# Fourteen projection panels computed channel-major in a hybrid attention/SSD/delta-rule layer

## The chip, the cores and the metric

The kernel runs on one core of one Trainium2 chip. The metric is the device time of one execution in microseconds (us). Engines are named as the profile names them: PE is TensorE, with PEld for its weight loads; DVE is VectorE; ACT is ScalarE; POOL is GpSimd; SP issues the weight DMAs. In a matmul the *stationary* operand (up to 128 columns) is loaded into the array first, and the *moving* operand (up to 512 columns) streams past it.

## The reference

One layer with three groups of heads, on 256 tokens of width 4096 (float32):

```python
h = rms_norm(x, norm_w)
proj = einsum('bsd,de->bse', h, w_in)               # 4096 -> 14392
(fox_qkv, fox_f, fox_z, ssd_xbc, ssd_z, ssd_dt, gdn_qkv, gdn_z, gdn_beta, gdn_a) = split(proj)
o_fox = forgetting attention of fox_qkv, gated by silu(fox_z)
xbc = silu(causal_depthwise_conv(ssd_xbc, ssd_conv_w) + ssd_conv_b)   # 4 taps along the tokens
o_ssd = chunked state-space scan of xbc, gated by silu(ssd_z)
qkv = silu(causal_depthwise_conv(gdn_qkv, gdn_conv_w))                # 4 taps along the tokens
o_gdn = chunked gated delta rule of qkv, gated by silu(gdn_z)
return x + concat(o_fox, o_ssd, o_gdn) @ w_out
```

The causal convolution works on each channel by itself: out[t] = w3 x[t] + w2 x[t-1] + w1 x[t-2] + w0 x[t-3].

## The kernel before

**The projection.** The 14392 output columns are 28 panels of 512 (`UNITS`) and 56 narrow gate columns. The contraction over 4096 has 32 steps `k` (`KT`) of 128. Operands are float32, split into a high and a low part in float32r (fp32r), which the PE takes in one pass; a product is then three matmuls: high x high, low x high, high x low. The input is split once into 32 tiles `xhl[k]` of [128 channels, 2 parts, 256 tokens]. The weights arrive by SP's queue, two steps in a DMA, and are split step by step: ACT writes `wh` (`split_w`, L189), DVE writes `wl` (L190); each has five buffers. In `product` (L193) the stationary operand is a [128 channels, 128 tokens] piece of `xhl[k]` and the moving one the 512 weight columns. So a panel's result stands token-major in two PSUM banks of [128 tokens, 512 channels], one for each half of the tokens.

**Panels.** `first_panels` (L243) does the first two panels (gq0, gk0) and the gate columns together, while the input still arrives. Each further panel is one call of `panel` (L204). The bank pool `psproj` has three banks, a panel uses two. When a panel is done, `take` (L936) reads both banks out on ACT, with the tokens' factor `rstd` of the RMS norm as a factor for each partition, and `unit_done` puts the panel's further work, a generator, into the queue `prep`. `panel` calls `drive` after each step, which lets the generators go on by one piece: so the later stages (convolution, attention, scans) are strewn among the products of the next panels. Last come eight output panels (`wo`) by the same `panel`, with `mix_split` for its left operand; they aren't touched. A scheduler decides from the program's order and its own estimate the order on each engine; on the chip each engine goes through its list in order.

**The convolution.** 14 of the 28 panels go through `conv_unit` (L389): gq, gk, gv of three groups, sB, sC and three sx. As the panel is token-major and the convolution runs along the tokens, eight 128x128 transposes on the PE (L397) first turn it into channel-major form in PSUM (`cps`). Then, for each of four channel tiles, ACT multiplies by the last tap (L404) and DVE adds the three shifted products (L407), both reading PSUM.

**The norm.** `input_norm` (L292), behind the first two panels, sums the squares over the channels by one matmul (`xnps`) and gets `rstd` by a chain of small DVE operations. `take` of the first panels waits for it.

Of the kernel before, what the change touches and what calls it, by code (L numbers as in the profile page):

```python
# [19 lines left out]
P = 128  # L20
D = 4096
T = 256
# [65 lines left out]
def tile_hybrid(ctx: ExitStack, tc: tile.TileContext, x, xT, w, wo, prm, cst, lev, out):  # L88
# [52 lines left out]
    def split_tile(k, name):  # L141
        return cp.tile([P, 2, T], F32R, tag=f"xhl{k}", name=f"{name}{k}")

# [49 lines left out]
    def product(ps, t, wh, wl, k):  # L193

        for tb in range(2):
# [3 lines left out]
            nc.tensor.matmul(ps[tb], h, wl, start=False, stop=k == KT - 1)  # L199

    def w_tile():
        return wp.tile([P, CK, 512], F32, tag="wr", name="wr", bufs=4)

    def panel(src, lhs):  # L204

        ps = [pp.tile([P, 512], F32, tag="proj", name="proj") for _ in range(2)]
        for c in range(0, KT, CK):
            wr = w_tile()
            nc.sync.dma_start(out=wr, in_=src[:, c:c + CK, :])
            for j in range(CK):  # L210
                wh, wl = split_w(wr[:, j, :])
                product(ps, lhs(c + j), wh, wl, c + j)
                drive()
        return ps

    def gate_chunk(ps, k0):

        n = GK_STEP
        gr = t2([P, n, NG], name="gwr")
        nc.sync.dma_start(out=gr, in_=w[0:P * WG].rearrange("(p j n) -> p j n", p=P, n=NG)[:, k0:k0 + n, :])  # L220
        gw = r4([P, n, 2 * NG], F32R, name="gw", tag="raw")
        nc.scalar.copy(gw[:, :, 0:NG], gr)
        nc.vector.tensor_tensor(out=gw[:, :, NG:2 * NG], in0=gr, in1=gw[:, :, 0:NG].bitcast(F32), op=ALU.subtract)
        for j in range(n):
            k = k0 + j
            nc.tensor.matmul(ps[0:2 * NG, :], gw[:, j, :], xhl[k].rearrange("p a t -> p (a t)"),  # L226
                             start=k == 0, stop=k == KT - 1)

    def gate_columns(ps):

        gs = t2([P, 2, T], name="gsum")
        nc.scalar.copy(gs[0:2 * NG, :, :], ps[0:2 * NG, :].rearrange("p (a t) -> p a t", a=2))
        o = bank("gtok")
        for tb in range(2):
            for i in range(2):
                nc.tensor.matmul(o[:, tb * NG:tb * NG + NG], gs[0:2 * NG, i, tb * P:tb * P + P],
                                 cst_s[0:2 * NG, M_GS:M_GS + NG], start=i == 0, stop=i == 1)
        raw["gates"] = cp.tile([P, 2, NG], F32, name="graw")
        for tb in range(2):
            nc.scalar.activation(raw["gates"][:, tb, :], o[:, tb * NG:tb * NG + NG], AF.Copy,  # L240
                                 scale=st["rstd"][:, tb:tb + 1])

    def first_panels(srcs):  # L243
# [4 lines left out]
        for c in range(0, KT, CK):  # L248
# [9 lines left out]
            for j in range(CK):  # L258
# [7 lines left out]
                for i in range(len(srcs)):  # L266
                    wh, wl = split_w(wr[i][:, j, :])
                    product(ps[i], xhl[k], wh, wl, k)
            if (c + CK) % GK_STEP == 0:
# [22 lines left out]
    def input_norm():  # L292
# [8 lines left out]
        affine(ss, v4(ps[:, 0:T], 2)[:, :, 0], 1.0 / D, EPS)  # L301
        st["rstd"] = rsqrt(ss, 2, "xn", 1)

    def const_tiles():
# [12 lines left out]
    def gates():  # L317
# [32 lines left out]
                                       op0=ALU.max, op1=ALU.add)  # L350
        ga = cp.tile([P, 2, NSP], F32, name="ga")
        nc.vector.tensor_tensor(out=ga, in0=spl, in1=mid(ea, 2), op=ALU.mult)
# [36 lines left out]
    def conv_unit(src, cw, dst, bias=None):  # L389

        acc = r4([P, 4, T], name="acc")
        for pr in range(2):
            ps = bank("cps")
            for i in range(2):
                ct = 2 * pr + i
                for tb in range(2):
                    nc.tensor.transpose(ps[:, i * T + tb * P:i * T + tb * P + P],  # L397
                                        src[:, tb, ct * P:ct * P + P], ident)
            for i in range(2):
                ct = 2 * pr + i  # L400
                q = ps[:, i * T:(i + 1) * T]
                wc = [prm_s[:, cw + ct * 4 + j:cw + ct * 4 + j + 1] for j in range(4)]
                b = 0.0 if bias is None else prm_s[:, bias + ct:bias + ct + 1]
                nc.scalar.activation(acc[:, ct, :], q, AF.Identity, scale=wc[3], bias=b)  # L404
                for j in (2, 1, 0):
                    s = 3 - j
                    nc.vector.scalar_tensor_tensor(out=acc[:, ct, s:], in0=q[:, 0:T - s], scalar=wc[j],  # L407
                                                   in1=acc[:, ct, s:], op0=ALU.mult, op1=ALU.add)
                yield 2
        if isinstance(dst, list):  # L410
# [522 lines left out]
    def unit_src(i):  # L933
        return w[P * (WG + i * WU):P * (WG + (i + 1) * WU)].rearrange("(p j n) -> p j n", p=P, n=512)

    def take(i, ps):  # L936
        name = UNITS[i][0]
        raw[name] = r4([P, 2, 512], name=f"raw_{name}", tag="raw")
        for tb in range(2):
            nc.scalar.activation(raw[name][:, tb, :], ps[tb], AF.Copy, scale=st["rstd"][:, tb:tb + 1])  # L940
        unit_done(name)
# [8 lines left out]
    for i in range(2, len(UNITS)):  # L950
        take(i, panel(unit_src(i), lambda k: xhl[k]))

# [72 lines left out]
```

## Time and profile before

| | before |
|---|---|
| time, median of 3 runs | 1756.83 us (1756.27 to 1756.95) |
| the profiled execution | 1756.48 us; its span, first to last instruction, 1754.7 us |
| PE busy | 1743.5 us, 99% |
| PEld (weight loads) busy | 1437.4 us, 82% |
| DVE busy | 1129.4 us, 64% |
| ACT busy | 954.5 us, 54% |
| granted PE clock | 1.00 |

Busy time is the time in which at least one instruction of the engine was under way. Matmuls overlap in the array, so a matmul's duration is longer than the distance to the next one; where the price of a matmul is wanted, starts are compared. Weight loads overlap matmuls and one another.

### The profile page before, as it was taken

Reading aid. Unit: us, or ns where it says so; the run is one execution under the profiler, and the core shown is the slowest. Engines: PE = TensorE matmul, PEld = TensorE weight load, DVE = VectorE, ACT = ScalarE, POOL = GpSimd, SP = SyncE. Lnnn points to the kernel's source line nnn. Section 1 sums busy time; section 2 is a strip of 40 time slices with the busy share of each in tenths; the row PEclk is TensorE's granted clock in tenths of the full one; section 3 lists DMA queues with packets and bytes.
Section 4 is the critical chain, followed back from the end, with each engine's and each line's share of the span. In section 5 each row is a group of like instructions: output and inputs, shape, how many; then the busy total and the mean of one; then the engine's idle time right before and its main releaser. Section 6 shows DMA issues by size and latency. Waiting matters only on the chain.

```text
span 1754.7 us, 24331 instructions
## 1 busy us (share of the span) xinstructions
PE 1743.5 (99%) x8368; PEld 1437.4 (82%) x8368; DVE 1129.4 (64%) x2111; ACT 954.5 (54%) x1678; POOL 133.3 (8%) x124
## 2 busy tenths in 40 slices
PE   8999999999999999999999999999999999999999
PEld 6888888888888888888888888888888888888887
DVE  8567767677677677575666765555655665555554
ACT  8456655455555555455555655556555754444443
POOL 0000200002000110002324100010000000000000
PEclk9999999999999999999999999999999999999999
DMA  8655555555555555555555566665666577777674
GB/s 318 187 169 181 161 174 156 157 170 159 175 147 163 159 170 166 146 168 166 169 168 162 175 191 182 190 182 168 181 190 182 172 235 215 215 215 214 202 204 138
DMA packets 90267, 317.73 MB, mean 181 GB/s; under 512 B 10016, under 2 KB 11040, under 8 KB 90144
## 3 DMA queue, kind: packets, MB, share of 16 engines
q1 hardware_dynamic: 83808, 302.94, 58.4%
q10 hardware_dynamic: 6336, 13.24, 2.1%
q8 instruction: 65, 1.06, 0.2%
q14 instruction: 58, 0.48, 0.1%
HBM read 311.95 MB, written 4.19 MB: 180 GB/s over the span
## 4 chain that ended last, share of the span: by engine, by line
PE 99%; ACT 0%; DMA 0%; DVE 0%; issue 0%; ACTq 0%
PE proj L197 30%; PE proj L199 30%; PE proj L198 30%; PE cps L397 1%; PE kkps L543 1%; PE yp L746 1%; PE yps L523 0%; PE zps L523 0%; PE zqs L523 0%; PE gproj L226 0%; PE mps L435 0%; PE cor L523 0%; PE o L523 0%; PE atps L523 0%; PE vn L523 0%; PE dps L383 0%
## 5 line engine op out<-in xcount | busy, mean ns | idle before, releaser
L190 DVE TENSOR_TENSOR wl<-wr,wh 128x512 fp32r<-128x512 f32 x1152 | 817.8, 720 | 539.6 <-ACT wh L189 479.2
L189 ACT CAST wh<-wr 128x512 fp32r<-128x512 f32 x1152 | 708.5, 621 | 705.3 <-DVE wl L190 362.1
L197 PE MATMUL proj<-wh,xhl 128*128 128x512 f32 x1792 | 710.5, 397 | 6.8 <-ACT wh L189 6.8
L198 PE MATMUL proj<-wh,xhl 128*128 128x512 f32 x1792 | 705.5, 394 | 0.0
L199 PE MATMUL proj<-wl,xhl 128*128 128x512 f32 x1792 | 693.5, 395 | 0.0
L197 PEld LDWEIGHTS proj<-wh,xhl 128*128 128x128 f32 x1792 | 337.4, 188 | 77.4 <-ACT wh L189 7.6
L198 PEld LDWEIGHTS proj<-wh,xhl 128*128 128x128 f32 x1792 | 337.4, 188 | 71.0
L199 PEld LDWEIGHTS proj<-wl,xhl 128*128 128x128 f32 x1792 | 336.6, 188 | 71.1
L197 PE MATMUL proj<-wh,mhl 128*128 128x512 f32 x512 | 200.8, 393 | 0.5 <-ACT wh L189 0.5
L198 PE MATMUL proj<-wh,mhl 128*128 128x512 f32 x512 | 199.9, 391 | 0.0
L199 PE MATMUL proj<-wl,mhl 128*128 128x512 f32 x512 | 196.5, 392 | 0.0
L197 PEld LDWEIGHTS proj<-wh,mhl 128*128 128x128 f32 x512 | 96.2, 188 | 21.6 <-ACT wh L189 1.2
L199 PEld LDWEIGHTS proj<-wl,mhl 128*128 128x128 f32 x512 | 96.2, 188 | 21.4
L198 PEld LDWEIGHTS proj<-wh,mhl 128*128 128x128 f32 x512 | 96.2, 188 | 21.1
L407 DVE SCALAR_TENSOR_TENSOR acc<-cps,prm_s,acc 128x255 f32<-128x255 f32 (+2 forms) x168 | 75.6, 476 | 9.5 <-ACT acc L404 8.8
L377 POOL TENSOR_TENSOR G<-cst_s,gh 128x384 fp32r<-128x384 f32 (+1 forms) x22 | 20.8, 947 | 230.3 <-DVE gh L354 120.5
L404 ACT ACTIVATE acc<-cps,prm_s 128x256 f32<-128x256 f32 x56 | 27.5, 510 | 13.9 <-PE cps L397 7.7
L588 DVE TENSOR_TENSOR tn<-tn,zps 128x512 f16<-128x512 f16 (+1 forms) x36 | 24.6, 683 | 4.4 <-PE zps L523 4.4
L597 POOL TENSOR_TENSOR res<-cst_s,tn 128x512 f32<-128x512 f32 x6 | 7.7, 1296 | 240.0 <-DVE tn L588 236.5
L377 POOL TENSOR_TENSOR G<-cst_s,gl 128x384 fp32r<-128x384 f32 (+1 forms) x22 | 25.3, 1152 | 0.2 <-PE dps L383 0.2
L589 DVE TENSOR_TENSOR tt<-tt,zqs 128x512 f16<-128x512 f16 (+1 forms) x36 | 24.5, 681 | 0.0
L579 ACT CAST y<-yps 128x512 f16<-128x512 f32 x36 | 19.4, 587 | 5.0 <-PE yps L523 4.9
(298 smaller groups left out, 935.4 us busy)
## 6 DMA issues: line engine op xcount, KB each, us to landing
wr<-in_w SPq DMA_DIRECT2D x446, 512.0 KB, 3.6
wr<-in_wo SPq DMA_DIRECT2D x128, 512.0 KB, 3.6
xres<-in_x ACTq DMA_DIRECT2D x16, 256.0 KB, 3.3
out<-xres ACTq DMA_DIRECT2D x16, 256.0 KB, 4.1
xr<-in_xT ACTq DMA_DIRECT2D x7, 514.0 KB, 5.2
wr<-in_w SPq DMA_DIRECT2D x4, 256.0 KB, 4.8
gwr<-in_w SPq DMA_DIRECT2D x4, 224.0 KB, 4.8
xr<-in_xT ACTq DMA_DIRECT2D x1, 385.5 KB, 4.6
```

The source lines that it names most:

```text
L189: nc.scalar.copy(wh, wr)
L190: nc.vector.tensor_tensor(out=wl, in0=wr, in1=wh.bitcast(F32), op=ALU.subtract)
L197: nc.tensor.matmul(ps[tb], h, wh, start=k == 0, stop=False)
L198: nc.tensor.matmul(ps[tb], lo, wh, start=False, stop=False)
L199: nc.tensor.matmul(ps[tb], h, wl, start=False, stop=k == KT - 1)
L377: nc.gpsimd.tensor_tensor(out=g[i], in0=mid(U, n), in1=bc(src[:, tb, c0:c0 + n].bitcast(F32), P), op=ALU.mult)
L397: nc.tensor.transpose(ps[:, i * T + tb * P:i * T + tb * P + P], src[:, tb, ct * P:ct * P + P], ident)
L404: nc.scalar.activation(acc[:, ct, :], q, AF.Identity, scale=wc[3], bias=b)
L407: nc.vector.scalar_tensor_tensor(out=acc[:, ct, s:], in0=q[:, 0:T - s], scalar=wc[j], in1=acc[:, ct, s:], op0=ALU.mult, op1=ALU.add)
L579: nc.scalar.copy(y[tb], v4(ps))
L588: nc.vector.tensor_tensor(out=tn2, in0=tn[tb], in1=v4(zp), op=ALU.subtract)
L589: nc.vector.tensor_tensor(out=tt2, in0=tt[tb], in1=v4(zq), op=ALU.subtract)
```

## The change

For the 14 panels that go through the convolution the operands of the product change places: 128 weight columns are stationary and the 256 tokens are moving (`product_t`). A step then has four channel tiles with three matmuls of 256 columns each. The result is channel-major at once: a bank holds two channel tiles of [128 channels, 256 tokens]. The transposes fall away, and the convolution reads the panel from SBUF.

Two things follow. A bank now holds two accumulations side by side. The first matmul of each bank is therefore 512 columns wide: it moves the high part of the tokens and 256 zeros behind it, for which tile 0 of the input has a third, cleared part (`x0z`). And `rstd` is now needed along the free axis: `input_norm` makes it into a row that is the same in all partitions (`rrow`), by scaling the identity on DVE, one fp32 matmul with ones, and a copy on ACT. `take` multiplies the banks by this row on DVE in place of ACT's scaled copy. Some gate tiles move from the constant pool to a rotating one.

```diff
     def split_tile(k, name):
-        return cp.tile([P, 2, T], F32R, tag=f"xhl{k}", name=f"{name}{k}")
+        if k:
+            return cp.tile([P, 2, T], F32R, tag=f"xhl{k}", name=f"{name}{k}")
+        t = cp.tile([P, 3, T], F32R, tag="xhl0", name=f"{name}0")
+        if name == "xhl":
+            nc.vector.memset(t[:, 1, :].bitcast(F32), 0.0)
+            st["x0z"] = t[:, 0:2, :]
+        return t[:, 0:3:2, :]
...
+    def product_t(ps, t, wh, wl, k):
+        xh, xl = t[:, 0, :], t[:, 1, :]
+        for ct in range(4):
+            o = ps[ct // 2][:, ct % 2 * T:ct % 2 * T + T]
+            h, lo = (v[:, ct * P:ct * P + P] for v in (wh, wl))
+            if k == 0 and ct % 2 == 0:
+                nc.tensor.matmul(v4(ps[ct // 2], 2), h, st["x0z"], start=True, stop=False)
+            else:
+                nc.tensor.matmul(o, h, xh, start=False, stop=False)
+            nc.tensor.matmul(o, h, xl, start=False, stop=False)
+            nc.tensor.matmul(o, lo, xh, start=False, stop=k == KT - 1 and ct % 2 == 1)
...
-    def panel(src, lhs):
+    def panel(src, lhs, mul=product):
...
-                product(ps, lhs(c + j), wh, wl, c + j)
+                mul(ps, lhs(c + j), wh, wl, c + j)
...
-                    product(ps[i], xhl[k], wh, wl, k)
+                    product_t(ps[i], xhl[k], wh, wl, k)
...
         st["rstd"] = rsqrt(ss, 2, "xn", 1)
+        dg = t2([P, 2, P], name="rdiag")
+        for tb in range(2):
+            nc.vector.tensor_scalar_mul(dg[:, tb, :], ident, st["rstd"][:, tb:tb + 1])
+        ps = bank("rrow")
+        nc.tensor.matmul(ps[:, 0:T], ones, dg.rearrange("p a b -> p (a b)"), start=True, stop=True)
+        st["rrow"] = cp.tile([P, T], F32, name="rrow")
+        nc.scalar.copy(st["rrow"], ps[:, 0:T])
...
     def conv_unit(src, cw, dst, bias=None):
         acc = r4([P, 4, T], name="acc")
-        for pr in range(2):
-            ps = bank("cps")
-            for i in range(2):
-                ct = 2 * pr + i
-                for tb in range(2):
-                    nc.tensor.transpose(ps[:, i * T + tb * P:i * T + tb * P + P],
-                                        src[:, tb, ct * P:ct * P + P], ident)
...
-                q = ps[:, i * T:(i + 1) * T]
+        for ct in range(4):
+            q = src[:, ct, :]
...
+    CONV = ("gq", "gk", "gv", "sB", "sC", "sx")
+
     def take(i, ps):
         name = UNITS[i][0]
-        raw[name] = r4([P, 2, 512], name=f"raw_{name}", tag="raw")
-        for tb in range(2):
-            nc.scalar.activation(raw[name][:, tb, :], ps[tb], AF.Copy, scale=st["rstd"][:, tb:tb + 1])
+        if name[:2] in CONV:
+            raw[name] = r4([P, 4, T], name=f"raw_{name}", tag="raw")
+            for b in range(2):
+                nc.vector.tensor_tensor(out=raw[name][:, 2 * b:2 * b + 2, :], in0=v4(ps[b], 2), in1=mid(st["rrow"], 2),
+                                        op=ALU.mult)
+        else:
+            raw[name] = r4([P, 2, 512], name=f"raw_{name}", tag="raw")
+            for tb in range(2):
+                nc.scalar.activation(raw[name][:, tb, :], ps[tb], AF.Copy, scale=st["rstd"][:, tb:tb + 1])
...
-        take(i, panel(unit_src(i), lambda k: xhl[k]))
+        take(i, panel(unit_src(i), lambda k: xhl[k], product_t if UNITS[i][0][:2] in CONV else product))
```

How the instructions move is shown at two places. The first is the PE's list in panel gv0, the third panel, whose first bank is served alone for some steps, as the second is still to be read out. A row is a line of the kernel, the operation, out<-in by the program's names, and the columns. Before, one half of the tokens for the steps 0 to 3:

```order
L197 MATMUL proj<-wh,xhl_90 128x512
L198 MATMUL proj<-wh,xhl_90 128x512
L199 MATMUL proj<-wl,xhl_90 128x512
L197 MATMUL proj<-wh,xhl_119 128x512
L198 MATMUL proj<-wh,xhl_119 128x512
L199 MATMUL proj<-wl,xhl_119 128x512
```

After, the first two channel tiles for the steps 0 and 1:

```order
L216 MATMUL proj<-xhl_90,wh 128x512
L219 MATMUL proj<-xhl_90,wh 128x256
L220 MATMUL proj<-xhl_90,wl 128x256
L218 MATMUL proj<-xhl_90,wh 128x256
L219 MATMUL proj<-xhl_90,wh 128x256
L220 MATMUL proj<-xhl_90,wl 128x256
L218 MATMUL proj<-xhl_132,wh 128x256
L219 MATMUL proj<-xhl_132,wh 128x256
L220 MATMUL proj<-xhl_132,wl 128x256
L218 MATMUL proj<-xhl_132,wh 128x256
L219 MATMUL proj<-xhl_132,wh 128x256
L220 MATMUL proj<-xhl_132,wl 128x256
```

Three matmuls of 512 columns have become six of 256, and at step 0 the first of the bank is 512 wide.

The second place is DVE's list when the first two panels go to their convolutions. `wl` is the split of a weight step, `acc` an operation of the convolution, `raw_gq` and `raw_gk` the reading of a bank, `be`, `pre`, `g_ab`, `gl` gate values. Before, where the first operations of the convolution stand:

```order
L357 TENSOR_TENSOR gl<-ga,gh 128x88
L190 TENSOR_TENSOR wl<-wr,wh 128x512 x4
L407 SCALAR_TENSOR_TENSOR acc<-cps,prm_s,acc 128x255 x2
L407 SCALAR_TENSOR_TENSOR acc<-cps,prm_s,acc 128x254 x2
L407 SCALAR_TENSOR_TENSOR acc<-cps,prm_s,acc 128x253
L190 TENSOR_TENSOR wl<-wr,wh 128x512
L407 SCALAR_TENSOR_TENSOR acc<-cps,prm_s,acc 128x253
L190 TENSOR_TENSOR wl<-wr,wh 128x512
```

After, the rows right behind the row of rstd (five steps of gv0 have been split ahead of it):

```order
L326 TENSOR_SCALAR rdiag<-cst_s,xn_y 128x128 x2
L963 TENSOR_TENSOR raw_gq_1444<-proj,rrow 128x512 x2
L963 TENSOR_TENSOR raw_gk_1447<-proj,rrow 128x512 x2
L348 TENSOR_TENSOR pre<-graw,prm_s 128x88
L427 SCALAR_TENSOR_TENSOR acc<-raw_gq_1444,prm_s,acc 128x255 x2
L387 TENSOR_SCALAR be<-be 128x24
L427 SCALAR_TENSOR_TENSOR acc<-raw_gq_1444,prm_s,acc 128x255 x2
L350 TENSOR_SCALAR pre<-pre 128x2x8
L427 SCALAR_TENSOR_TENSOR acc<-raw_gq_1444,prm_s,acc 128x254
L197 TENSOR_TENSOR wl<-wr,wh 128x512
L427 SCALAR_TENSOR_TENSOR acc<-raw_gq_1444,prm_s,acc 128x254
```

The readings of the first two panels have come into DVE's list, and five operations of the convolution stand between them and the next split; five more and two gate operations stand between that split and the one after, three more before the third.

## Rows read from the trace of the kernel before

**Rows 1.** The page: busy time of the engines; the granted clock in 40 slices.

```profile
PE 1743.5 (99%) x8368; PEld 1437.4 (82%) x8368; DVE 1129.4 (64%) x2111; ACT 954.5 (54%) x1678; POOL 133.3 (8%) x124
PEclk9999999999999999999999999999999999999999
```

**Rows 2.** The page: the chain of work that ended last, by line.

```profile
PE proj L197 30%; PE proj L199 30%; PE proj L198 30%; PE cps L397 1%; PE kkps L543 1%; PE yp L746 1%; PE yps L523 0%; PE zps L523 0%; PE zqs L523 0%; PE gproj L226 0%; PE mps L435 0%; PE cor L523 0%; PE o L523 0%; PE atps L523 0%; PE vn L523 0%; PE dps L383 0%
```

**Rows 3.** Groups by line: count, busy us, mean ns, idle before.

```profile
L190 DVE TENSOR_TENSOR wl<-wr,wh 128x512 fp32r<-128x512 f32 x1152 | 817.8, 720 | 539.6 <-ACT wh L189 479.2 <-PE proj L198 25.8 <-PE proj L199 19.6
L197 PE MATMUL proj<-wh,xhl 128*128 128x512 f32 x1792 | 710.5, 397 | 6.8 <-ACT wh L189 6.8
...
5.70 0.80 PE L197 MATMUL proj<-wh,xhl 128*128 128x512 f32 x1 [5.70 <-ACT wh L189]
```

**Rows 4.** Timeline of the PE near 800 us: start, duration; 22 products.

```profile
801.03 0.39 PE L197 MATMUL proj<-wh,xhl 128*128 128x512 f32 x1
...
805.83 0.39 PE L197 MATMUL proj<-wh,xhl 128*128 128x512 f32 x1
```

**Rows 5.** Groups by line and shape: the transposes, one of six groups.

```profile
L397 PE MATMUL cps<-cst_s,raw_sx 128*128 128x128 f32 x24 | 3.9, 272 | 0.0
```

**Rows 6.** Timeline of the PE around one set of four transposes.

```profile
783.52 0.60 PE L397 MATMUL cps<-cst_s,raw_sx 128*128 128x128 f32 x4
...
784.20 0.40 PE L198 MATMUL proj<-wh,xhl 128*128 128x512 f32 x1
```

**Rows 7.** Timeline: weight loads under short matmuls; a run of 128-column fp32 matmuls.

```profile
107.89 1.09 PEld L236 LDWEIGHTS gtok<-cst_s,gsum 112*128 112x128 f32 x8
108.12 1.00 PE L236 MATMUL gtok<-cst_s,gsum 112*128 112x56 f32 x8
108.91 0.19 PEld L197 LDWEIGHTS proj<-wh,xhl 128*128 128x128 f32 x1
...
500.06 1.95 PE L523 MATMUL atps<-tn,m 128*128 128x128 f32 x16
```

**Rows 8.** Timeline of the PE: fp32r matmuls of 384 and 512 columns among products, two in each place.

```profile
851.19 0.34 PE L382 MATMUL dps<-G,slr 128*128 128x384 f32 x1
...
851.54 0.40 PE L197 MATMUL proj<-wh,xhl 128*128 128x512 f32 x1
...
199.52 0.40 PE L382 MATMUL dps<-G,slr 128*128 128x512 f32 x1
...
200.00 0.39 PE L197 MATMUL proj<-wh,xhl 128*128 128x512 f32 x1
```

**Rows 9.** Timeline of the PE: four records of fp32 matmuls of 256 columns.

```profile
189.07 1.02 PE L543 MATMUL kkps<-kq 128*128 128x256 f32 x4
```

**Rows 10.** Groups by line and shape, DVE and ACT.

```profile
L407 DVE SCALAR_TENSOR_TENSOR acc<-cps,prm_s,acc 128x254 f32<-128x254 f32 x56 | 26.3, 476 | 0.2
L153 DVE SCALAR_TENSOR_TENSOR xhl<-xr,xhl 128x256 fp32r<-128x256 f32 x32 | 14.2, 483 | 3.6 <-ACT xhl L152 3.6
L495 DVE TENSOR_TENSOR kn<-kps,rsqk_y 128x512 f32<-128x512 f32 x6 | 3.9, 685 | 0.1
L903 DVE COPY fot<-ofp 128x128 f32<-128x128 f32 x16 | 4.6, 288 | 3.6 <-ACT osq L902 3.6
L447 ACT ACTIVATE mix<-mps,prm_s 128x256 f32<-128x256 f32 x24 | 9.8, 473 | 1.2 <-PE mps L435 1.1
L940 ACT ACTIVATE raw_gk<-proj,xn_y 128x512 f32<-128x512 f32 x6 | 4.0, 693 | 0.6 <-PE proj L199 0.6
```

**Rows 11.** Timeline: the first reading behind the norm, and the PE's next product.

```profile
107.87 1.27 ACT L940 ACTIVATE raw_gq<-proj,xn_y 128x512 f32<-128x512 f32 x2 [2.84 <-DVE xn_y L285]
...
108.93 0.47 PE L197 MATMUL proj<-wh,xhl 128*128 128x512 f32 x1
```

**Rows 12.** Timeline of DVE: five convolution operations and three splits, in a row.

```profile
127.34 2.04 DVE L407 SCALAR_TENSOR_TENSOR acc<-cps,prm_s,acc 128x255 f32<-128x255 f32 x5 [1.22 <-ACT acc L404]
...
137.76 1.90 DVE L190 TENSOR_TENSOR wl<-wr,wh 128x512 fp32r<-128x512 f32 x3 [2.04 <-ACT wh L189]
```

More of the change, by code (lines that the diff above doesn't have):

```diff
@@ L225, in gate_chunk @@
             k = k0 + j
-            nc.tensor.matmul(ps[0:2 * NG, :], gw[:, j, :], xhl[k].rearrange("p a t -> p (a t)"),
-                             start=k == 0, stop=k == KT - 1)
+            nc.tensor.matmul(v4(ps, 2)[0:2 * NG], gw[:, j, :], xhl[k], start=k == 0, stop=k == KT - 1)
     def gate_columns(ps):
@@ L237, in gate_columns @@
                                  cst_s[0:2 * NG, M_GS:M_GS + NG], start=i == 0, stop=i == 1)
-        raw["gates"] = cp.tile([P, 2, NG], F32, name="graw")
+        raw["gates"] = t2([P, 2, NG], name="graw")
         for tb in range(2):
@@ L350, in gates @@
                                        op0=ALU.max, op1=ALU.add)
-        ga = cp.tile([P, 2, NSP], F32, name="ga")
+        ga = t2([P, 2, NSP], name="ga")
         nc.vector.tensor_tensor(out=ga, in0=spl, in1=mid(ea, 2), op=ALU.mult)
@@ L391, in conv_unit @@
         acc = r4([P, 4, T], name="acc")
-        for pr in range(2):
-            ps = bank("cps")
-            for i in range(2):
-                ct = 2 * pr + i
-                for tb in range(2):
-                    nc.tensor.transpose(ps[:, i * T + tb * P:i * T + tb * P + P],
-                                        src[:, tb, ct * P:ct * P + P], ident)
-            for i in range(2):
-                ct = 2 * pr + i
-                q = ps[:, i * T:(i + 1) * T]
[L402 to L409, printed above, removed]
+        for ct in range(4):
+            q = src[:, ct, :]
+            wc = [prm_s[:, cw + ct * 4 + j:cw + ct * 4 + j + 1] for j in range(4)]
+            b = 0.0 if bias is None else prm_s[:, bias + ct:bias + ct + 1]
+            nc.scalar.activation(acc[:, ct, :], q, AF.Identity, scale=wc[3], bias=b)
+            for j in (2, 1, 0):
+                s = 3 - j
+                nc.vector.scalar_tensor_tensor(out=acc[:, ct, s:], in0=q[:, 0:T - s], scalar=wc[j],
+                                               in1=acc[:, ct, s:], op0=ALU.mult, op1=ALU.add)
+            yield 1
         if isinstance(dst, list):
```

## The prediction

> **What bounds the kernel now.** The first view to read is the page's busy list with the clock's slices [rows 1]: TensorE (PE) is busy for 99% of the span, at a granted clock of nine tenths or more in every slice (2.4 GHz, the higher of its two levels), while VectorE (DVE) is at 64% and ScalarE (ACT) at 54%. The second view is the chain that ended last [rows 2]: 90% of it are the three product lines L197 to L199 on the PE, 1% the transposes L397. The third is the groups by line [rows 3]: before L197 the PE stood idle 6.8 us in all, of which one wait of 5.7 us is the start. So the end moves by what the PE's own instructions take, one after another, and work on DVE or ACT counts only where it makes the PE wait. A busy time there (397 ns for one matmul) is no price, since matmuls overlap. The price is the distance between starts, which the timeline gives: between the two rows of [rows 4] lie 21 matmuls in 4.80 us, **0.2286 us for 512 columns**. 512 columns at 2.4 GHz are 0.2133 us, so 0.0153 us are something else. What that is decides this case.
>
> **The change part by part.**
>
> *Transposes removed.* 14 panels had eight each, 112 in all, in six groups of which [rows 5] shows one. [rows 6] show four of them between products: from the start of the first (783.52) to the start of the second product behind them (784.20) are 0.68 us, less one product 0.2286, which leaves 0.451 us for four. 28 times this is **-12.6 us**, all on the path.
>
> *Products in another shape.* Before, a step k of a panel is 6 matmuls of 512 columns; 14 panels of 32 steps make 2688, or 614.5 us. After, it is 12 of 256 columns, with a weight load each; two per panel (28) are 512 wide, as they also clear a bank. So 5348 narrow ones and 28 wide ones (6.4 us). The columns are the same but for these 28. The time depends on a narrow one's price, which no row shows, as the trace has no such fp32r matmul of 256 columns. Each 0.001 us of it is 5.3 us at the end.
> - If the 0.0153 us grows with the columns, a narrow one takes half, 0.1143 us.
> - If it is a fixed price of each matmul, it takes 0.2286 less 256/2.4 GHz, 0.1219 us.
> - A weight load can't be hidden below its own pace. [rows 7] show it: eight loads of 128 columns run under matmuls of only 56 columns, and from the row of 108.12 (where the second load starts, one product after the first) to the next line's load at 108.91 are 7 loads in 0.79 us, 0.113 us each; the 16 fp32 matmuls of 128 columns take (1.95 - 0.275)/15 = 0.1117 us. That is the floor, even if the stream itself cost nothing beyond its columns (0.107).
>
> The rows nearest in kind are fp32r matmuls of 384 columns [rows 8]: two of them take 0.35 us from the first start to the next product's, 0.175 each; two of 512 columns in the same place take 0.48, or 0.24 each. From the product's 0.2286 to 0.175 are 0.0536 us for 128 columns, from the 0.24 of the same line 0.065; a price that grows with columns asks for 0.0571, a fixed one for 0.0533. The rows of one line have all in common but the columns, so I hold with the first, but times are printed to 0.01 us and this doesn't settle it. I take 0.1145: half of the wide one, just above the load's floor. 5348 x 0.1145 + 6.4 - 614.5 = **+4.2 us**. The ends are 0.1117 (-10.7 us) and 0.1219 (+43.8 us).
>
> The Trainium skill (TensorE: Matmul & The Clock Gate, Back-to-back issue gap) gives a warm matmul as N/2.4 GHz plus 2.5 ns, which would be 0.216 us for 512 columns and 0.109 for 256. The trace has 0.2286 for 512, so for these operands the rule is 6% short. By the rule the narrow product would fall under the pace of its weight load.
>
> *The row of rstd.* One fp32 matmul of 256 columns (two records) is added between two stages: four such records take 1.02 us with a last one of 0.378 [rows 9], 0.214 each, **+0.4 us**. In front of it are two small scalings on DVE, behind it a copy on ACT.
>
> *Reading a panel out.* 28 ACT readings of 0.69 us become 28 DVE multiplications of the same shape; the nearest row is kn, also 128x512 from PSUM by a broadcast, 0.685 busy and 0.6 from start to start. The convolution's 168 DVE and 56 ACT operations now read SBUF: L407 takes 0.476 us and L153, the same operation on SBUF with 256 columns, 0.483 [rows 10]. So they cost about what they did. DVE gains 17 us, ACT loses 19. All this is priced at nothing where weights are split ahead of the PE: at each later panel end DVE has split four steps of the next panel (of five buffers) before it turns to the readings, which gives the PE 4 x 1.37 = 5.5 us. The readings and the fifth split take 1.8 us of it.
>
> *The first convolutions.* Here the cover is thin. Both first panels must be read out together, and now this waits for the row of rstd. In [rows 11] ACT reads out from 107.87, released by the end of the chain of small DVE operations, and the PE, after 15 products and gtok, goes on at 108.93 without waiting. After: two scalings (0.25 each, taken near the 0.288 of L903 [rows 10]) to 108.35, the matmul to about 109.0 with its latency, the ACT copy (0.47, L447) to 109.5, the first half of the reading at 110.15. The PE has the same columns as before up to gtok at 108.12 [rows 7], waits 0.25 for the scalings, then has 0.43 + 0.9 for gtok, and stands until 110.15: 0.7 us. Then it has five split steps (both halves of the second bank, 3.5 us, to 113.7). DVE has four readings to 111.9 and then the order shown above: 5 conv operations (0.39 each from start to start [rows 12]) and three gate operations before the next split, which lands near 115.2; five conv operations and two gate ones before the one after (118.4); three before the third (120.2). Each is late by what the PE has not spent waiting already: about 1.0, 1.5 and 0.4 us. Before, four splits stand ahead of the first conv operation and the splits go on among the next ones, so nothing was late. **+3.6 us** in all; the ends are 0 (ACT and DVE start earlier) and 7 (each conv operation at its full 0.476).
>
> *Nothing.* The clearing of one 128x256 tile at the start precedes the first product, which waits 5.7 us for a weight cast; the gate tiles change pools only; the gate product keeps its 32 matmuls.
>
> **The sum.** -12.6 + 4.2 + 0.4 + 3.6 = -4.4 us. The profiled execution took 1756.5 us (span 1754.7); the median of the runs is 1756.8, which is the same for this purpose. So 1752.2 us.
>
> **The rivals.**
> 1. *A fixed price of each matmul, slower.* Place: each of 5348 narrow products. For it: 0.0536 above is nearly its 0.0533, and each product has a load of its own. Against: fp32 records of 256 columns at two cycles each take 0.214 [rows 9] for 0.2133 of streaming, with the same load under them, so a load alone doesn't cost 0.015. Time: 1756.5 - 12.6 + 43.8 + 4.0 = 1792. From 0.1153 us for a narrow product on, there is no gain left.
> 2. *The load's pace is the bound.* The extra of the wide ones goes away in short ones, and 0.1117 remains: 1756.5 - 12.6 - 10.7 + 4.0 = 1737. Against: 0.175 for 384 columns still holds 0.015 beyond 0.160. The rule of the Trainium skill quoted above leads to this time.
> 3. *DVE becomes the bound at each conv panel's end.* In the order after, gv0 has nine conv operations in a row ahead of a split: 1.2 + 0.6 + 3.5 + 0.6 = 5.9 us against five split steps, 6.9 us. If ACT's first convolution step or the release of the five buffers eats that 1.0 us, the PE stands about 1.2 us at each of 13 panels: 1752 + 16 = 1768. Against: DVE is idle 540 us before its splits, 479 of them for ACT [rows 3].
> 4. *Loads don't overlap.* A load's record lasts 0.188 us and they fill 82% of the span [rows 1]. If a narrow product had to wait for a whole record, 5348 x 0.188 + 6.4 - 614.5 = +397 us, 2145 us. Against: [rows 7], where loads follow at 0.113. The Trainium skill (Perfetto Trace Analysis, Identifying the Most-Contended Engine) judges the PE by this very share; here records would add up to more than the span, and the trace shows why that can be.
>
> **How the numbers follow.** The forecast has 0.55; its own range is 1745 to 1761 (narrow product 0.1135 to 0.116, first convolutions 0 to 7 us). Rival 1 has 0.22, rival 2 0.08, rival 3 0.12, rival 4 0.03. The range 1737 to 1792 goes from rival 2 to rival 1 and leaves out rival 4 and what lies beyond these two, about 0.12. 0.2%, or 3.5 us, is what a measurement of this kernel can tell from none. Faster: 0.36 of the forecast and rival 2, 0.44. Same: 0.16 of the forecast and 0.04 of rival 3, 0.20. Slower: the rest, 0.36.
>
> **What would show it.** The timeline inside gk or gv panels: narrow products 0.1145 apart, or 0.112, or 0.122. No L397 group, and total PE busy without gaps except at 108 to 122 us, where the split (wl, line 197 of the changed kernel) should be named as what the PE waits for. Readings of about 0.68 us on DVE (its line 963) with idle time ahead of them; waits of PE for wl at later panel ends would mean rival 3. Weight load records that start 0.11 apart speak against rival 4. The prediction is wrong above all if the narrow product is not near 0.1145.

## The result and the profile after

The changed kernel takes **1788.05 us** (median; 1787.64 to 1788.56), the kernel before 1756.89 in the same comparison: a ratio of **1.0179 (95% interval 1.0166 to 1.0191)**, slower by 31.2 us. The forecast was 1752.2. The profiled execution has a span of 1785.8 us.

The page of the changed kernel, busy list and chain by line, answers to [rows 1, 2]:

```profile
PE 1773.5 (99%) x10946; PEld 1565.8 (88%) x10946; DVE 1152.2 (65%) x2142; ACT 940.3 (53%) x1652; POOL 135.8 (8%) x124
...
PE proj L204 18%; PE proj L206 18%; PE proj L205 18%; PE proj L219 12%; PE proj L220 12%; PE proj L218 12%; PE kkps L563 1%; PE yp L766 1%; PE zps L543 0%; PE yps L543 0%; PE proj L216 0%; PE zqs L543 0%; PE gproj L247 0%; PE mps L455 0%; PE cor L543 0%; PE o L543 0%
```

TensorE (PE) is the bound as before, at 99%, and the transposes are gone from the chain. The waits in the view by engine (what waited, for what, us in total, times, longest), the first row from the kernel of before, the others from the changed kernel:

```profile
PE proj L197 <- ACT wh L189: 7.4, 3, 5.7
...
PE proj L216 <- DVE xsq L173: 5.6, 1, 5.6
PE proj L220 <- DVE wl L197: 1.5, 2, 1.2
PE proj L216 <- DVE raw_gq L963: 0.4, 1, 0.4
```

The longest is the start in both, 5.7 us before [rows 3] and 5.6 after; in all there are 7.4 us of waits before and 7.5 after. So 31 us came without a wait to show for them, and must lie in the distance between starts. The timeline of the PE in the changed kernel gives it as [rows 4] did (start, duration). First 41 distances of narrow products in a convolution panel, then 21 of wide products in a panel that the diff doesn't touch:

```profile
798.75 0.28 PE L220 MATMUL proj<-xhl,wl 128*128 128x256 f32 x1
...
803.60 0.28 PE L219 MATMUL proj<-xhl,wh 128*128 128x256 f32 x1
...
913.29 0.40 PE L204 MATMUL proj<-wh,xhl 128*128 128x512 f32 x1
...
918.19 0.40 PE L204 MATMUL proj<-wh,xhl 128*128 128x512 f32 x1
```

The narrow ones stand 4.85/41 = 0.1183 us apart, where 0.1145 was forecast. The surprise is the second pair: 4.90/21 = **0.2333 us** for the very product that took 4.80/21 = 0.2286 before. Over all neighbouring products of a shape in the traces, the mean distance of wide ones is 229.1 ns before and **233.3 ns** after, and of narrow ones 118.3 ns; all such means below are taken this way. Groups by line put 3 x 896 and 3 x 512 wide products on the untouched panels, 4224; each of them became 4.2 ns slower:

- untouched products: 4224 x (233.26 - 229.09) ns = **+17.6 us**
- products in another shape: 5348 x 118.26 ns + 28 x 233.3 ns - 2688 x 229.09 ns = 632.5 + 6.5 - 615.8 = **+23.2 us**
- transposes -12.6, row of rstd +0.4, first convolutions about +2.1 (below), and -1.7 for the waits behind the start that only the kernel of before has

That is 29.0 of the 31.2 us. Of the other 2, about 1 stands behind the last product: from its start to the end of the span the traces have 4.21 us before and 5.17 after. Why that is, and where the rest lies, is not known. The clock doesn't enter: the granted clock is 1.0 of 2.4 GHz in both.

### The profile page after: what moved, and what is told of

It is laid out like the page before. It is cut to its first block, busy times and chain, and to the rows that moved or that the text cites. A ratio compares the mean times of both kernels' runs of the same rounds, so it can differ in the third digit from the quotient of the medians.

```text
span 1785.8 us, 29514 instructions
## 1 busy us (share of the span) xinstructions
PE 1773.5 (99%) x10946; PEld 1565.8 (88%) x10946; DVE 1152.2 (65%) x2142; ACT 940.3 (53%) x1652; POOL 135.8 (8%) x124
## 4 chain that ended last, share of the span: by engine, by line
PE 99%; DVE 0%; DMA 0%; issue 0%; ACT 0%; DVEq 0%
PE proj L204 18%; PE proj L206 18%; PE proj L205 18%; PE proj L219 12%; PE proj L220 12%; PE proj L218 12%; PE kkps L563 1%; PE yp L766 1%; PE zps L543 0%; PE yps L543 0%; PE proj L216 0%; PE zqs L543 0%; PE gproj L247 0%; PE mps L455 0%; PE cor L543 0%; PE o L543 0%
## 5 line engine op out<-in xcount | busy, mean ns | idle before, releaser
L219 PE MATMUL proj<-xhl,wh 128*128 128x256 f32 x1792 | 504.2, 283 | 0.0
L220 PE MATMUL proj<-xhl,wl 128*128 128x256 f32 x1792 | 497.7, 283 | 1.6 <-DVE wl L197 1.5
L218 PE MATMUL proj<-xhl,wh 128*128 128x256 f32 x1764 | 498.8, 284 | 0.0
L204 PE MATMUL proj<-wh,xhl 128*128 128x512 f32 x896 | 359.2, 401 | 0.0
L205 PE MATMUL proj<-wh,xhl 128*128 128x512 f32 x896 | 354.9, 396 | 0.0
L206 PE MATMUL proj<-wl,xhl 128*128 128x512 f32 x896 | 348.2, 397 | 0.0
L219 PEld LDWEIGHTS proj<-xhl,wh 128*128 128x128 f32 x1792 | 339.0, 189 | 0.7
L220 PEld LDWEIGHTS proj<-xhl,wl 128*128 128x128 f32 x1792 | 334.5, 189 | 3.6 <-DVE wl L197 2.2
L218 PEld LDWEIGHTS proj<-xhl,wh 128*128 128x128 f32 x1764 | 333.1, 189 | 0.6
L206 PEld LDWEIGHTS proj<-wl,xhl 128*128 128x128 f32 x896 | 167.9, 188 | 40.2
L204 PEld LDWEIGHTS proj<-wh,xhl 128*128 128x128 f32 x896 | 168.1, 188 | 39.2
L205 PEld LDWEIGHTS proj<-wh,xhl 128*128 128x128 f32 x896 | 168.2, 188 | 39.1
```

What stands on the lines that cost most here:

```text
L204: nc.tensor.matmul(ps[tb], h, wh, start=k == 0, stop=False)
L205: nc.tensor.matmul(ps[tb], lo, wh, start=False, stop=False)
L218: nc.tensor.matmul(o, h, xh, start=False, stop=False)
L219: nc.tensor.matmul(o, h, xl, start=False, stop=False)
L220: nc.tensor.matmul(o, lo, xh, start=False, stop=k == KT - 1 and ct % 2 == 1)
```

## The experiments

What could slow products that nobody touched? The change also moves buffers. Tile 0 of the tokens grows by a third part of 1024 bytes, the tile `rrow` (1024 bytes) is new, and `graw` and `ga` (800 bytes together) leave the pool of constants. All of these lie ahead of the weights' ring in SBUF, and only the first ahead of the other token tiles. So the distance from a token tile to a weight tile, of which one moves through the array while the other is loaded, changed by 1248 - 1024 = 224 bytes. In the built programs it is 64 modulo 256 bytes before and 32 after. **Theory P**: this distance sets the pace of the products, narrow and wide. **Theory Q**: the changed program is slower in itself; the narrow products, more instructions and more loads, hold up the wide ones between them too. The distances named below are those of weights from tokens modulo 256 bytes.

**1. The kernel of before with the changed kernel's places.** No product is changed:

```diff
-        return cp.tile([P, 2, T], F32R, tag=f"xhl{k}", name=f"{name}{k}")
+        if k:
+            return cp.tile([P, 2, T], F32R, tag=f"xhl{k}", name=f"{name}{k}")
+        return cp.tile([P, 3, T], F32R, tag="xhl0", name=f"{name}0")[:, 0:2, :]
...
-        raw["gates"] = cp.tile([P, 2, NG], F32, name="graw")
+        raw["gates"] = t2([P, 2, NG], name="graw")
...
+        pad = cp.tile([P, T], F32, name="pad")
+        nc.gpsimd.memset(pad[:, 0:1], 0.0)
...
-        ga = cp.tile([P, 2, NSP], F32, name="ga")
+        ga = t2([P, 2, NSP], name="ga")
```

> The kernel before with nothing changed but where tiles lie in SBUF: tile 0 of the input has a third part that nobody uses, the gate tiles come from the rotating pool and an unused tile stands in for the row of rstd, so that every input tile, wh and wl lie at the addresses of the changed kernel. Theory P (the places set the pace): in the changed kernel the untouched products of 512 columns are 0.2332 us apart, before they were 0.2291, because the operands moved; then all 6912 products here slow down by 0.0041 us, about +28 us, 1785 us. Rival Q (the narrow products, or the longer program, slow the PE down also for the others): no change, 1757 us, products 0.229 us apart.

Measured: **1784.12 us**, ratio 1.0154 (1.0138 to 1.0169), 27 us slower than before with the instructions of before. Its timeline, 21 distances of wide products in the same place as [rows 4]:

```profile
798.79 0.40 PE L200 MATMUL proj<-wh,xhl 128*128 128x512 f32 x1
...
803.69 0.39 PE L200 MATMUL proj<-wh,xhl 128*128 128x512 f32 x1
```

4.90/21 = 0.2333 us, the pace of the changed kernel's wide products. Q falls, and the places of the buffers are shown to set the pace of the wide products. That it is the distance, as P says, and not each place by itself is left to experiment 4. For 6912 products the 4.2 ns make 28.9 us, a little more than the 27.3 measured.

**2. The changed kernel with the distance of before.** One unused tile of 32 bytes ahead of `rrow`:

```diff
         st["rstd"] = rsqrt(ss, 2, "xn", 1)
+        pad = cp.tile([P, 8], F32, name="pad")
+        nc.gpsimd.memset(pad[:, 0:1], 0.0)
```

> The changed kernel with an unused tile of 32 bytes ahead of the weight pools, so that wh, wl and the input tiles lie at the same remainders of 256 bytes as before the change. Theory P, if it is the low address bits: the 4224 untouched wide products go back to 0.229 us (-17 us), the narrow ones from 0.118 to between 0.115 and 0.118 (0 to -18 us): 1753 to 1771 us. Theory P with higher address bits, and rival Q: 1788 us as it was.

Measured: **1755.19 us**, ratio 0.9991 (0.9982 to 1.0001); 32 unused bytes give back 33 us. Its timeline: 21 distances of wide products, then 41 distances of narrow ones in one panel, then, in another panel, 23 ahead of the wide product that opens its second bank and 19 behind it:

```profile
363.16 0.39 PE L204 MATMUL proj<-wh,xhl 128*128 128x512 f32 x1
...
367.97 0.39 PE L205 MATMUL proj<-wh,xhl 128*128 128x512 f32 x1
...
129.82 0.28 PE L218 MATMUL proj<-xhl,wh 128*128 128x256 f32 x1
...
134.47 0.28 PE L219 MATMUL proj<-xhl,wh 128*128 128x256 f32 x1
...
317.73 0.28 PE L219 MATMUL proj<-xhl,wh 128*128 128x256 f32 x1
...
320.44 0.28 PE L218 MATMUL proj<-xhl,wh 128*128 128x256 f32 x1
320.56 0.39 PE L216 MATMUL proj<-xhl,wh 128*128 128x512 f32 x1
320.79 0.28 PE L219 MATMUL proj<-xhl,wh 128*128 128x256 f32 x1
...
322.94 0.28 PE L220 MATMUL proj<-xhl,wl 128*128 128x256 f32 x1
```

Wide: 4.81/21 = 0.2290, as before. Narrow: 4.65/41 = 0.1134 in the first panel; in the other 2.71/23 = 0.1178 and then, with one wide product between, 2.15/19 = 0.1132. So the distance isn't all: products at one distance, with the same lines in the same order, hold two paces. In the whole trace, of the uninterrupted runs of 14 or more narrow products (no other matmul and no distance above 0.18 us between them), 60 are near 0.1134 and 41 near 0.1178, and none changes its pace on the way; the next run may have the other. The mean over the kernel is 115.1 ns, against the 114.5 of the forecast.

**3. Half the columns, without the change.** The kernel of before, its places untouched; in the 14 panels the tokens stay stationary, and the weights move in halves of 256 columns:

```diff
+            for c in range(2):
+                cs = slice(c * T, c * T + T)
+                o = ps[tb][:, cs]
...
+                    nc.tensor.matmul(o, h, wh[:, cs], start=False, stop=False)
+                nc.tensor.matmul(o, lo, wh[:, cs], start=False, stop=False)
+                nc.tensor.matmul(o, h, wl[:, cs], start=False, stop=k == KT - 1 and c == 1)
```

> The kernel before, tokens stationary as they were, transposes kept, but in the 14 panels the 512 weight columns are moved in two halves of 256, each with a load of its own: 5320 narrow matmuls in place of 2660 wide ones, at the old places in SBUF. It prices the narrow product alone. If a narrow one costs half of a wide one (0.1145): 1758 us. If it costs what the changed kernel shows (0.1183): +20 us, 1777 us. If the extra is a fixed price of each matmul (0.1219): +40 us, 1797 us.

Measured: **1771.38 us**, ratio 1.0083 (1.0066 to 1.0100). The narrow products have a mean of 117.3 ns and the untouched wide ones keep 229.1. 5320 x 117.29 + 28 x 229.1 - 2688 x 229.09 ns = +14.6 us, and 14.6 were measured. More and shorter products beside them did not slow the wide ones, the second blow to Q. The mean of the narrow ones is 2.2 ns above experiment 2's, but that is no price of moving the weights: the trace holds the same two paces, 92 such runs near 0.1178 us and 10 near 0.1134, so the slow one is only more frequent here.

**4. A table of paces.** A kernel of stretches of 24 products each: `abuf` stationary, `bbuf` moving, the place of one or the other shifted in bytes.

```diff
+            s = sta[:, s0 + i % pieces * 128:s0 + i % pieces * 128 + cols]
+            m = mov[:, m0 + i // 2 % 4 * 512:m0 + i // 2 % 4 * 512 + n]
+            nc.tensor.matmul(o[0:cols, 0:n], s, m, start=i in (0, 3), stop=i >= count - 6 and i % 3 == 2)
```

> A table in place of the kernel (none of the layer is computed): stretches of 24 fp32r matmuls in a row, one stretch for each count of moving columns (512 down to 128), each offset of moving and stationary operand in SBUF (0 to 256 bytes), fewer stationary columns, and fp16 and fp32 beside them. If the extra grows with columns: 512 columns 0.229, 384 0.172, 256 0.115 us. If it is fixed: 0.229, 0.176, 0.122. If places matter (P), stretches of the same shape at other offsets differ by some 0.004 us; if only the program around it matters (Q), all offsets agree within 0.001. If the load steals from the stream, 32 or 64 stationary columns are faster than 128.

Its timeline, a row for each stretch. In `wap` and `nap` both operands stand alike; `waq` and `naq` have the stationary one 32 bytes on, `wcp` and `ncp` the moving one, `wcq` both; `wep` has the moving one 64 bytes on, `wgp` 256. `lb` to `le` are fp32r too, with fewer moving columns, `ca` and `cc` have 64 stationary columns, `ha` and `hb` are fp16, `ta` is fp32:

```profile
42.55 5.61 PE L55 MATMUL wap<-bbuf,abuf 128*128 128x512 f32 x24
48.00 5.76 PE L55 MATMUL waq<-bbuf,abuf 128*128 128x512 f32 x24
...
64.83 5.76 PE L55 MATMUL wcp<-bbuf,abuf 128*128 128x512 f32 x24
70.43 5.61 PE L55 MATMUL wcq<-bbuf,abuf 128*128 128x512 f32 x24
...
87.03 5.67 PE L55 MATMUL wep<-bbuf,abuf 128*128 128x512 f32 x24
...
109.30 5.63 PE L55 MATMUL wgp<-bbuf,abuf 128*128 128x512 f32 x24
...
120.37 3.02 PE L55 MATMUL nap<-bbuf,abuf 128*128 128x256 f32 x24
123.23 2.99 PE L55 MATMUL naq<-bbuf,abuf 128*128 128x256 f32 x24
126.06 2.96 PE L55 MATMUL ncp<-bbuf,abuf 128*128 128x256 f32 x24
...
136.68 4.33 PE L55 MATMUL lb<-bbuf,abuf 128*128 128x384 f32 x24
140.85 3.67 PE L55 MATMUL lc<-bbuf,abuf 128*128 128x320 f32 x24
144.36 2.82 PE L55 MATMUL ld<-bbuf,abuf 128*128 128x192 f32 x24
147.02 2.81 PE L55 MATMUL le<-bbuf,abuf 128*128 128x128 f32 x24
...
156.51 5.68 PE L55 MATMUL ca<-bbuf,abuf 128*64 128x512 f32 x24
...
167.60 2.89 PE L55 MATMUL cc<-bbuf,abuf 128*64 128x256 f32 x24
...
194.92 2.78 PE L55 MATMUL hb<-hbuf 128*128 128x256 f16 x24
197.54 10.53 PE L55 MATMUL ta<-raw,raw 128*128 128x256 f32 x48
```

A row holds 23 distances and one last record (0.39 us with 512 columns, 0.28 with 256). At distance 0: (5.61 - 0.39)/23 = 0.227 us. One operand 32 bytes on, either one: (5.76 - 0.39)/23 = 0.2335. Both 32 bytes on: 0.227 again. 64 bytes: (5.67 - 0.39)/23 = 0.2296; 256 bytes: 0.228. So not the place but the distance counts, and the table has the 229 of before and the 233 of after. No other engine is busy beside these products, but for two DVE copies of 0.16 us in each stretch, so it is not ACT's and DVE's writing of the weight tiles either. Narrow: 0.119 at 0, 0.1178 with the stationary one (the weights, in the changed kernel) 32 bytes on, 0.1165 with the moving one.

The table also answers what the prediction left open, at distance 0: from one start to the next row's, 384 columns take 4.17/24 = 0.174 us, 320 take 0.146, 192 take 2.66/24 = 0.111, and 128 the same, as their durations of 2.82 and 2.81 show. Beyond the columns at 2.4 GHz these are 0.014, 0.013 and, with the 0.2133 and 0.1067 of 512 and 256 columns, 0.014 and 0.012: **a nearly fixed price of each product**, down to the pace of the loads. A load of half the columns doesn't take it away from 512 columns (`ca`, 0.230), but it takes about half of it from 256: `cc`, with 64 stationary columns, has (2.89 - 0.28)/23 = 0.1135 us, where 128 have 0.119. So the load has a part in the narrow product's price.

**5, 6 and 7. Which distance is best, and for whom.** The first table has 512 columns fastest at 0 and 256 columns slowest there. The kernel of before got an unused tile of 192 bytes, the changed kernel one of 224 (in the place of experiment 2's); either makes the distance 0. With them ran a second table, in the kernel's triples, in which the weights' buffer steps on by 32 bytes from stretch to stretch (`wa`, `wb`, ... wide, `na`, `nb`, ... narrow, 48 products each).

```diff
         st["rstd"] = rsqrt(ss, 2, "xn", 1)
+        pad = cp.tile([P, 48], F32, name="pad")
+        nc.gpsimd.memset(pad[:, 0:1], 0.0)
```

That is the edit of the kernel before; the changed kernel has 56 for 48. In the second table, `r` goes from 0 to 120 elements in steps of 8:

```diff
+            w, wl = (B[:, r + p * 1536:][:, 0:512] for p in range(2))
+            return (h, w), (lo, w), (h, wl)
...
+            h, lo = (B[:, r + p * 1536 + i % 4 * 128:][:, 0:128] for p in range(2))
+            return (h, xh), (h, xl), (lo, xh)
```

> The kernel of before with an unused tile of 192 bytes ahead of the later buffers: the weights of a product stand at the same place modulo 256 bytes as the tokens, where in the kernel of before they stand 64 bytes on. Nothing else is changed. If the pace goes by the distance of the two operands as in the table of places (226.7 ns at distance 0 against 229.5 at 64), all 6912 wide products lose about 2.4 ns and the kernel about 16 us: 1740, faster than both. If the table's single stretches do not carry over to the kernel's own mix of operands, the time stays at 1757, or goes wherever the mix puts it; within 0.2% of 1757 says that.

> The changed kernel with an unused tile of 224 bytes instead of 32, so that the two operands of a product stand at the same place modulo 256 bytes. By the table of places the 4252 wide products take 226.7 ns instead of 229.1 (about 10 us less than with the pad of 32 bytes), and the 5348 narrow ones 119.4 instead of 115.1 (about 23 us more): about 1768. If the place that suits the wide products suits the narrow ones too: about 1745. If places stopped mattering, 1755 again.

> A table of paces alone; it computes none of the layer. Products in the kernel's own triples (high by high, low by high, high by low), wide ones with 512 moving columns and narrow ones with 256, each in 16 stretches in which the weights buffer steps on by 32 bytes. If the pace goes by the distance of the operands, the wide stretches run between 226.7 and 236 ns, with 229 at 64 bytes and 233 at 32, and the narrow ones between 115 and 120, and the pattern repeats after 256 bytes. If the order of the operands or the buffers matters more than the distance, the stretches do not repeat and do not meet the kernel's own 229.1 at 64 bytes.

Measured: the kernel of before with its 192 bytes **1746.45 us**, ratio **0.9941** (0.9925 to 0.9958); the changed kernel with 224 bytes **1771.26 us**, ratio 1.0083 (1.0068 to 1.0098). The timeline of the former, 21 distances of wide products:

```profile
1649.68 0.39 PE L197 MATMUL proj<-wh,mhl 128*128 128x512 f32 x1
...
1654.44 0.39 PE L197 MATMUL proj<-wh,mhl 128*128 128x512 f32 x1
```

and of the latter, 41 distances of narrow ones:

```profile
799.84 0.28 PE L218 MATMUL proj<-xhl,wh 128*128 128x256 f32 x1
...
804.75 0.28 PE L218 MATMUL proj<-xhl,wh 128*128 128x256 f32 x1
```

Wide 4.76/21 = 0.2267, narrow 4.91/41 = 0.1198. The mean of wide ones is 227.5 in the first kernel, so it won 6912 x 1.57 ns = 10.9 us (measured 10.4; 16 were expected, from the table's 226.7 for all). In the second kernel wide ones have 227.3 and narrow ones 119.75: against experiment 2, -8.0 and +24.6 us, and 16.1 were measured.

The second table's timeline:

```profile
42.32 11.04 PE L36 MATMUL wa<-bbuf,abuf 128*128 128x512 f32 x48
53.20 11.37 PE L36 MATMUL wb<-bbuf,abuf 128*128 128x512 f32 x48
64.41 11.16 PE L36 MATMUL wc<-bbuf,abuf 128*128 128x512 f32 x48
...
131.44 11.05 PE L36 MATMUL wi<-bbuf,abuf 128*128 128x512 f32 x48
142.32 11.37 PE L36 MATMUL wj<-bbuf,abuf 128*128 128x512 f32 x48
...
220.56 5.91 PE L36 MATMUL na<-abuf,bbuf 128*128 128x256 f32 x48
...
231.98 5.82 PE L36 MATMUL nc<-abuf,bbuf 128*128 128x256 f32 x48
```

Over 47 distances: `wa` (0 bytes) 0.2266, `wb` (32) 0.2336, `wc` (64) 0.2291; `wi` and `wj`, 256 bytes behind `wa` and `wb`, are the same again. The other five wide stretches of the period lie at 0.2331 to 0.2341, so only 0 and 64 are good places among these steps. Here the table meets the kernels. In one point it doesn't: the narrow product at 64 bytes (`nc`) takes (5.82 - 0.28)/47 = 0.1179, the slower of the two paces in experiment 2; the faster one, 0.1134, appears in no stretch of 256 moving and 128 stationary columns. As a stretch is one uninterrupted run, it could show only one of the two; by this table alone the narrow product would gain 0.5 ns, and not 3.1, from 32 to 64 bytes.

**8. Each shape at its better place.** The changed kernel, the weights' tiles with 64 spare columns, in which wide panels put their columns at distance 0 and narrow ones at 64:

```diff
-    def split_w(wr):
+    def split_w(wr, o=0):
...
-        wh = wp.tile([P, 512], F32R, tag="wh", name="wh")
-        wl = wp.tile([P, 512], F32R, tag="wl", name="wl")
+        wh = wp.tile([P, 576], F32R, tag="wh", name="wh")[:, o:o + 512]
+        wl = wp.tile([P, 576], F32R, tag="wl", name="wl", bufs=4)[:, o:o + 512]
...
-                wh, wl = split_w(wr[:, j, :])
+                wh, wl = split_w(wr[:, j, :], 8 if mul is product_t else 56)
...
-                    wh, wl = split_w(wr[i][:, j, :])
+                    wh, wl = split_w(wr[i][:, j, :], 8)
```

> The changed kernel with 64 spare columns in each tile of the weights (ring of wl 4 instead of 5 to make the room), in which the channel-major panels put their columns 64 bytes on from the tokens' place modulo 256 bytes and the other panels at the tokens' own place. If the place of the two operands sets the pace and nothing else about them, the narrow products keep the 115.1 ns that they had with the pad of 32 bytes, and the 4252 wide ones fall from 229.1 to the 226.7 to 227.8 that the kernel of before has at that place: 1755.2 less 7 or 8 is about 1747, and the change, each way of multiplying at its better place, is worth nothing beside the kernel of before with its pad of 192 bytes (1746.5). If the narrow products' 115.1 came from something else than that distance (the ring's pitch, which is another here), they stand between 117 and 120 and the time between 1757 and 1775. A ring of 4 that is too short would show as waits of TensorE for wl at the ends of panels.

Measured: **1747.32 us**, ratio 0.9945 (0.9931 to 0.9958). Its timeline, 21 wide distances:

```profile
1650.39 0.39 PE L204 MATMUL proj<-wh,mhl 128*128 128x512 f32 x1
...
1655.15 0.39 PE L204 MATMUL proj<-wh,mhl 128*128 128x512 f32 x1
```

0.2267 us; the means are 227.3 ns for wide and 115.0 for narrow products, both as expected. Its waits are those of the changed kernel but for 1.2 us (rdiag 0.5, wh 0.4, wl 1.7 instead of 1.5, and 0.1 at the start), so the shorter ring holds. The time is what the theory gave, and it beats both kernels; so does experiment 5, with a smaller edit and no difference between the two that these runs could tell.

Put together, medians in us; where the operands lie decides what the change is worth. Only the 24.8 are far beyond the noise: at 64 bytes the interval reaches no difference, at 32 the intervals of the two kernels (against the kernel of before) still touch, and in the last row they nearly coincide:

| distance modulo 256 bytes | before's way | the change | the change's worth |
|---|---|---|---|
| 64 (before's own) | 1756.8 | 1755.2 | -1.6 |
| 32 (the change's own) | 1784.1 | 1788.05 | +3.9 |
| 0 | 1746.45 | 1771.3 | +24.8 |
| each shape at its better one | 1746.45 | 1747.3 | +0.9 |

## Why the prediction was wrong

**The step that failed is the one headed *Nothing*.** It said that "the gate tiles change pools only", priced the clearing of tile 0's third part by its instruction alone, and said nothing of the tile's new size; the new tile `rrow` was priced as a copy. As work they cost nothing. As bytes they moved the weights by 224 bytes against the tokens, and that costs 17.6 us on 4224 products which the forecast didn't count at all, and most of the next term's error. Experiment 1 shows it without the change, experiment 2 takes it back with the change in place. The diff holds the three sizes from which the shift is worked out. No row of before gives its price, as the panels of one kernel all have one distance, but one hints at it: the gate's products, also 512 columns wide, with weights at several other distances, stand (2.01 - 0.39)/7 = 0.2314 us apart, not 0.2286:

```profile
102.39 2.01 PE L226 MATMUL gproj<-xhl,gw 128*112 128x512 f32 x8
```

**The term *Products in another shape* was mis-sized:** +23.2 us for +4.2, as a narrow product took 118.3 ns instead of 114.5. At the distance from which its wide price was read, it takes 115.1 (experiment 2), so about 5348 x 3.1 ns = 17 us of the error of 19 come from the same shift, and 2 from the rule "half of the wide one". Whether the extra beyond the columns grows with them or is fixed, on which the forecast chose, has no single answer. At 0 bytes it is 13.9 ns wide and 13.1 narrow, fixed as rival 1 had it. At 64 bytes it is 15.8 wide and 8.4 narrow, near the forecast's half, but that is luck: the 8.4 is a mean over runs with 6.7 and runs with 11.1 ns, and neither is half.

**Rival 1** gave 1792, near the result, by another sum: its 43.8 us on the narrow products were 23.2, and it had nothing on the untouched ones. That its number came out is no proof of it. **Rival 2** asked for the loads' pace, which the table puts at 0.111 us; narrow products stayed above it in every kernel. The rule of the Trainium skill that led there (TensorE: Matmul & The Clock Gate, Back-to-back issue gap) gives 0.109 us for 256 columns: the table's fp16 products have it, 2.62/24 = 0.109, the fp32r ones never. **Rival 3** would show as waits for `wl` at later panel ends; the waits above have none. **Rival 4** is refuted by products 0.118 us apart.

**Right**, as far as a sum that leaves 2 us open can tell, were the transposes (-12.6) and the row of rstd. Right were also the readings at no price and the place and order of the stalls at the first convolutions. The timeline of the PE in the changed kernel (in brackets idle time and what ended it):

```profile
112.91 0.50 PE L216 MATMUL proj<-xhl,wh 128*128 128x512 f32 x1 [0.35 <-DVE raw_gq L963]
...
117.60 0.39 PE L220 MATMUL proj<-xhl,wl 128*128 128x256 f32 x1 [0.29 <-DVE wl L197]
...
120.45 0.39 PE L220 MATMUL proj<-xhl,wl 128*128 128x256 f32 x1 [1.17 <-DVE wl L197]
```

and of DVE there:

```profile
112.17 1.29 DVE L963 TENSOR_TENSOR raw_gq<-proj,rrow 128x512 f32<-128x512 f32 x2 [1.20 <-ACT rrow L330]
...
116.86 0.68 DVE L197 TENSOR_TENSOR wl<-wr,wh 128x512 fp32r<-128x512 f32 x1
...
119.72 0.68 DVE L197 TENSOR_TENSOR wl<-wr,wh 128x512 fp32r<-128x512 f32 x1
```

The PE waits for the reading, then for the two splits behind the convolution's operations: 0.35, 0.29 and 1.17 us, where 0.7, 1.0 and 1.5 were forecast; a third late split adds 0.26 between starts (0.4 forecast). Together 2.1 us for 3.6. In experiment 2 the view of waits has the same 0.4 and 1.5 us, and one more of 0.6 for `wh`; there the terms, less the 1.7 us of before's waits, add up to -4.6 us, and -1.6 were measured (the interval reaches to -3.2), so 1.4 to 3 us are not located, 1.0 of them again behind the last product.

## What to carry to other kernels

A change that resizes, adds or drops a buffer moves every buffer behind it, and a product's pace can hang on that: when a PE-bound kernel shifts by a per cent or two without a wait, compare the distance between starts in a panel that the change doesn't touch before explaining anything by the change. To judge the change itself, run both versions at the same distance of operands, or each at its best, by an unused tile of a few bytes; here 192 bytes were worth more (0.6%) than the whole rewrite. A price read from one shape is not a price for another: even at the same distance, the narrow product held two paces, neither of them half of the wide one's.

## What the runs showed of the hardware

- An fp32r product of 512 columns takes 226.7 to 234.1 ns in the second table, depending on the distance of its two operands in SBUF modulo 256 bytes; fp16 of 512 columns runs at (5.35 - 0.39)/23 = 0.216 us in the row of `ha` below. The Trainium skill (SBUF — State Buffer, Who interferes with whom) has a single rule, that engines contend only for the port pair of VectorE and GpSimd; by it experiment 1 would have stayed at 1756.8 us. It took 1784.1, and the measurement decides. That TensorE's own two streams, the operand that moves and the weights being loaded, get in each other's way is argued from the distance and not shown: no run took the loads away, and halving them helped 256 columns (0.119 to 0.1135 us) but not 512 (0.227 to 0.230) in experiment 4.

```profile
189.73 5.35 PE L55 MATMUL ha<-hbuf 128*128 128x512 f16 x24
```

- At 64 bytes, 256 columns have two paces, 0.1134 and 0.1178 us, whether the tokens move (experiment 2) or the weights (experiment 3). Each holds for a whole run of products and can change when another matmul comes between. The means of 115.1 and 117.3 ns differ by how often each pace comes; what picks between them stays open.
